# Two of the four blocks of v as seven block products, with gate blocks in their places, in a decoder layer

## The chip, the cores and the metric

The kernel runs on one core of one Trainium2 chip. The metric is the device time of one execution in microseconds (us), median of three runs; lower is better. The engines are called as the profile calls them: PE is TensorE (matmul), PEld its weight load, DVE VectorE, ACT ScalarE, POOL GpSimd, SP SyncE, which only issues DMAs here.

## The reference

One layer over x of 1024 tokens x 1024 channels, float32:

```
h = rms_norm(x, attn_norm_w)
q, k, v, u, g = split(h @ w_in)              # 1024, 1024, 1024, 2048, 2048 columns
q, k = rms_norm over each half head of 64    # 8 heads, two halves each
lam = exp(sum(lam_q1 * lam_k1)) - exp(sum(lam_q2 * lam_k2)) + lam_init
p = softmax(q1 k1' + bias) - lam * softmax(q2 k2' + bias)      # causal
y_a = (rms_norm(p @ v) * (1 - lam_init)) @ w_proj_attn
c = causal depthwise convolution of width 31 of (u_a * sigmoid(u_b))
y_b = silu(layer_norm(c)) @ w_proj_conv
x = x + (sigmoid(g_a) * y_a + sigmoid(g_b) * y_b) @ w_out
x = x + (silu(gate) * up) @ w_down           # gate, up from rms_norm(x), 2816 wide
```

## The kernel before

Every float32 matrix is split into a high part (rounded by ScalarE, `split_hi`, L120) and a low part (the rest, by VectorE in `split_lo`, L125, or by GpSimd in `low`, L131, while `low_by_pool` is set), and a product is three matmuls: high x high, high x low, low x high (L168 to L170). The projection of h is cut into items. `V0` to `V3` are the four blocks of 256 columns of v: per tile of 128 tokens 8 x 3 = 24 matmuls of 256 columns. `G0` to `G15` are blocks of 128 columns of the gates: per half of 512 tokens 24 matmuls of 512 columns. `Q0` to `Q7` are a head's q and k together, 256 columns like a V item. `U0` to `U7` are the convolution's input, two blocks of 128 columns each.

The program has stages. The **opening** (`opening`, from L1076) loads the tiles of x, normalises and turns them by matmuls with the identity (`turn_x`, L724), and does V0 and U0 in between. Its first instructions are three dummy matmuls (`keep_busy`, L208), the squares of the first tile in two halves (L699 on ScalarE, L700 on VectorE), the spreading of the norm's weight over the partitions by a matmul with a row of ones (L212, copied by L213), the norm (L714), three dummies again, and the split of V0's weights, which come in two DMAs of 512 KB (L1085). The lists `first` and `last` (L402, L403) then order the items: V1, V2 (`first`), then U1 to U7, then Q0, V3 (`last`). GpSimd sums the halves of h meanwhile into four matrices T1 to T4 (`sums_of_h`). The pairs U1 to U7 (`u_pair`) take their blocks by Winograd's form of Strassen's product: seven products of half-sized blocks (A11, A12, S1 to S4, A22 of the weights with h's quarters and T1 to T4) in place of eight, with the same weights prepared by `prepare` one item ahead, as a generator that is stepped between products.

**Attention** follows: 8 heads x 8 slots (`scores`, `turn`, `weigh`), and the lists in `later` say which items fill TensorE in which head: Q of the next head and one or two gate blocks; a generator is advanced by one group (an accumulation of one bank) per slot, and a head whose list has only one gate block leaves two slots without one. The convolution's 30 multiply-adds per block (`conv_taps`, L594, VectorE) run in the background: the loop at L1231 gives them 3.25 instructions per step of the first stage, and attention shares out the rest by its slack. q and k of a head are normalised over 64 channels (`rsq`: ScalarE's square root and VectorE's reciprocal for the first head, logarithm and exponential for the others), turned by TensorE (`turn_qk`, L815, named pQ) and partly moved between partitions by small DMAs (ks, qs; L826 to L837) before the first score (L1289, named sc). `make_neglam` computes lambda by an exponential at the start of attention, behind a load of ScalarE's table.

The rest of the layer (projections, layer norm, output product, feed-forward) is not touched. Tiles live in pools with rotating buffers, and the order of the instructions on each engine is fixed when the program is built, by a scheduler that starts from the order of the code.

## Time and profile before

| | |
|---|---|
| runs | 1730.33, 1729.57, 1726.5 us; median 1729.57 |
| the profiled execution's own time | 1735.99 us |
| its span, first to last instruction | 1734.2 us |
| mean granted TensorE clock | 0.998 |
| busy | PE 1718.1, PEld 1480.7, DVE 1286.8, ACT 862.0, POOL 219.1 us |
| opening, V1 starts at | 65.97 us |
| U pairs end, Q0 and V3 | 258.98 us |
| first score | 315.08 us |
| last score | 807.5 us |

The page gives the busy time of each engine and its share of the span. A row of the timeline has the start, the duration of the group, the engine, the line of the kernel, the operation, what it writes and reads, how many instructions it merges, and in brackets how long the engine had been idle and what ended that. A row of the windows view gives, for a stretch of the span, the busy microseconds of PE, PEld, DVE, ACT and POOL, each with its count of instructions, then the granted clock of TensorE, the share of the DMA engines and GB/s. A busy TensorE is not one at its peak: neighbouring matmuls overlap, so the pace is read from starts.

### The profile page before, as it was taken

What the parts mean: (1) busy time and instruction counts of PE and PEld (TensorE: products, weight loads), DVE (VectorE), ACT (ScalarE), POOL (GpSimd) and SP (SyncE); (2) the same over time, 40 slices, a digit from 0 to 9 for tenths busy, and PEclk for the clock granted to TensorE, in tenths of its full rate; (3) what the DMA queues carried; (4) which work ended last, traced back from release to release, by engine and by line L of the source; (5) the groups of instructions that cost most, each with busy time, mean ns of one, the idle gap of its engine ahead of it and who ended that gap; (6) DMA issues with size and microseconds to landing.
All of it is one profiled execution on the core that took longest, in us unless ns stands there. A gap on an engine that the chain in (4) does not pass through costs nothing.

```text
span 1734.2 us, 25866 instructions
## 1 busy us (share of the span) xinstructions
PE 1718.1 (99%) x9245; PEld 1480.7 (85%) x9245; DVE 1286.8 (74%) x2128; ACT 862.0 (50%) x1958; POOL 219.1 (13%) x207
## 2 busy tenths in 40 slices
PE   9899999999999999999999999999999999999999
PEld 7897889998998998988788888888888888888887
DVE  6785889898988888978587768966676667565554
ACT  5234334667777776755557324633333333333332
POOL 3988761000000000000000000000000000000000
PEclk9999999999999999999999999999999999999999
DMA  6244436436335444434973674235445444598663
GB/s 207 80 134 129 151 109 173 122 86 180 108 103 169 114 127 126 116 114 132 333 262 110 212 266 142 78 114 172 153 162 174 154 149 154 172 361 283 218 216 131
DMA packets 261603, 281.64 MB, mean 162 GB/s; under 512 B 16545, under 2 KB 181985, under 8 KB 261474
## 3 DMA queue, kind: packets, MB, share of 16 engines
q1 hardware_dynamic: 255360, 269.28, 48.1%
q0 software_dynamic: 5680, 9.39, 2.7%
q8 instruction: 73, 1.20, 0.3%
q10 hardware_dynamic: 434, 1.32, 0.2%
q14 instruction: 56, 0.46, 0.1%
HBM read 181.84 MB, written 85.50 MB: 154 GB/s over the span
## 4 chain that ended last, share of the span: by engine, by line
PE 94%; DVE 3%; DMA 2%; ACT 1%; issue 1%; SPq 0%; DVEq 0%; ACTq 0%
PE acc L980 30%; PE acc L488 12%; PE pg L168 12%; PE pg L169 12%; PE pg L170 12%; PE wo L1850 4%; PE sc L1289 2%; PE sc L1290 2%; PE pT L1328 2%; DVE acc L594 1%; PE pg L1106 1%; PE pW L168 1%; PE pW L169 1%; PE pW L170 1%; PE pQ L815 1%
## 5 line engine op out<-in xcount | busy, mean ns | idle before, releaser
L594 DVE SCALAR_TENSOR_TENSOR acc<-u,cw,acc 128x1023 f32<-128x1023 f32 (+14 forms) x240 | 303.4, 1264 | 25.2 <-ACT acc L588 22.6
L169 PE MATMUL pg<-wlo,hT_hi 128*128 128x256 f32 x704 | 200.9, 286 | 5.0 <-DVE wlo L125 5.0
L170 PE MATMUL pg<-whi,hT_lo 128*128 128x256 f32 x704 | 201.4, 286 | 0.0
L168 PE MATMUL pg<-whi,hT_hi 128*128 128x256 f32 x704 | 200.8, 286 | 0.4 <-DVE v L125 0.4
L125 DVE TENSOR_TENSOR wlo<-draw,whi 128x1024 fp32r<-128x1024 f32 x75 | 91.8, 1223 | 85.0 <-ACT whi L120 79.9
L120 ACT CAST whi<-draw 128x1024 fp32r<-128x1024 f32 x75 | 79.1, 1055 | 129.5 <-PE acc L488 116.0
L169 PEld LDWEIGHTS pg<-wlo,hT_hi 128*128 128x128 f32 x704 | 135.5, 192 | 7.3 <-DVE wlo L125 5.6
L168 PEld LDWEIGHTS pg<-whi,hT_hi 128*128 128x128 f32 x704 | 135.2, 193 | 2.1 <-DVE v L125 0.6
L170 PEld LDWEIGHTS pg<-whi,hT_lo 128*128 128x128 f32 x704 | 135.5, 192 | 1.7
L120 ACT CAST whi<-wraw 128x1024 fp32r<-128x1024 f32 x90 | 94.6, 1052 | 80.0 <-PE pg L169 31.1
L488 PE MATMUL acc<-wlo,whi 128*128 128x512 f32 x308 | 119.8, 389 | 0.0
L488 PE MATMUL acc<-whi,wlo 128*128 128x512 f32 x308 | 119.8, 389 | 0.0
L1296 ACT ACTIVATE E<-E,mn 128x640 f32<-128x640 f32 (+7 forms) x128 | 99.8, 781 | 30.5 <-DVE mn L1291 28.9
L168 PE MATMUL pg<-hT_hi,whi 128*128 128x512 f32 x288 | 114.4, 397 | 0.1
L169 PE MATMUL pg<-hT_lo,whi 128*128 128x512 f32 x288 | 113.7, 395 | 0.0
L170 PE MATMUL pg<-hT_hi,wlo 128*128 128x512 f32 x288 | 113.7, 395 | 0.0
L120 ACT CAST whi<-s 128x1024 fp32r<-128x1024 f32 x54 | 56.8, 1053 | 104.7 <-PE acc L980 101.7
L125 DVE TENSOR_TENSOR wlo<-wraw,whi 128x1024 fp32r<-128x1024 f32 x75 | 94.6, 1264 | 11.4 <-ACT whi L120 11.2
L1291 DVE CUSTOM_DVE_ANT_0 E<-sc,tb 128x512 f32<-128x512 f32 (+3 forms) x128 | 74.2, 585 | 33.3 <-PE pT L1328 16.0
L980 PE MATMUL acc<-h_hi,whi 128*128 128x512 f32 x240 | 93.4, 389 | 0.0
L980 PE MATMUL acc<-h_lo,whi 128*128 128x512 f32 x240 | 93.4, 389 | 0.0
L980 PE MATMUL acc<-h_hi,wlo 128*128 128x512 f32 x240 | 90.1, 389 | 0.0
(370 smaller groups left out, 4599.6 us busy)
## 6 DMA issues: line engine op xcount, KB each, us to landing
wraw<-in_w_gate_up_dram SPq DMA_DIRECT2D x44, 512.0 KB, 4.8
wraw<-in_w_in_dram SPq DMA_DIRECT2D x40, 512.0 KB, 4.1
qs<-qs SPq DMA_DIRECT2D x96, 128.0 KB, 2.3
wd<-in_w_down_dram SPq DMA_DIRECT2D x44, 256.0 KB, 3.2
tdT<-wd SPq DMA_DIRECT2D x88, 128.0 KB, 4.6
draw<-sdS SPq DMA_DIRECT2D x44, 256.0 KB, 3.8
draw<-tdT SPq DMA_DIRECT2D x44, 256.0 KB, 3.9
wraw<-in_w_in_dram SPq DMA_DIRECT2D x32, 256.0 KB, 3.3
```

The costliest lines, as they stand in the source:

```text
L120: act.copy(dst, src)
L125: last_lo[0] = dve.tensor_tensor(dst, src, f32(hi), op=ALU.subtract).ins
L168: pe.matmul(o, lh, rh, start=start, stop=False)
L169: pe.matmul(o, lh, rl, start=False, stop=False)
L170: last_mm[0] = pe.matmul(o, ll, rh, start=False, stop=stop).ins
L488: m = pe.matmul(o[s_][i][:], l_[:, ts], r_[:, 512:], start=start and j + y_ == 0, stop=j == n - 1 and y_ == 2, skip_group_check=not start,)
L594: dve.scalar_tensor_tensor(a_, us[c][:, : S - n], cw[:, c, t : t + 1], a_, op0=ALU.mult, op1=ALU.add)
L980: last_mm[0] = pe.matmul(o[:], a_[x_][:, k, :], b_[y_][:, k, :], start=start and k + x_ + y_ == 0, stop=k == 3 and x_ == 1, skip_group_che ...
L1289: pe.matmul(o[:, :w], qh[:, qs], k, start=True, stop=False)
L1291: dve.tensor_tensor_reduce(e[:, ks], o[:, :w], tb[:, S - nk + c0 : S - nk + c0 + w], 1.0, mn[:, j : j + 1] if c0 else 3.0e38, ALU.add, ALU ...
L1296: act.activation(e[:, :nk], e[:, :nk], AF.Exp, bias=mn[:, j : j + 1], scale=-1.0, accum_out=l[:, j : j + 1])
L1850: last_mm[0] = pe.matmul(o[s_][i][:], A[u_], B[v_], start=start and j + y_ == 0, stop=j == 3 and y_ == 2, skip_group_check=not start,).ins
```

## The change

Five things change.

- V2 and V3 leave the lists. `wide_pair` computes both together behind U7 as seven products of 512 tokens x 512 rows x 256 columns (`tall`), with weights from `wide_prepare` and the T matrices that the U pairs already use. Six PSUM banks serve as three pairs; ScalarE copies three partial sums out (L1091 of the changed kernel), VectorE adds three times two halves (L1098), and all eight halves are split and stored as before.
- G0 and G1 take V2's place in `first`, G2 and G3 take V3's in `last`; in attention each of the seven heads with a Q item has one gate block.
- The convolution's background steps are 3.0 per product in `wide_pair` and 1.5 per step of G2 and G3.
- V0's weights and the second tile of x are issued from ScalarE's queue, and one dummy matmul stands where the second three stood.
- The first head's q and k use logarithm and exponential; the logarithm's table is loaded, and lambda computed, ahead of Q0.

On ScalarE the program starts so before (xt is a tile of x, wraw the weights of V0, anw_b the norm's weight):

```order
L185 ACT_TABLE_LOAD
L199 DMA anw_b<-in_attn_norm_w_dram 1x1024
L202 DMA xt_102<-in_x_dram 128x512
L699 ACTIVATE xj_349,ssx_348<-xt_102 128x512
L190 DMA xt_354<-in_x_dram 128x1024
L190 DMA xt_356<-in_x_dram 128x1024
L652 ACTIVATE t_361<-v_358 128x1
```

and so after the change, on the same engine at the same place:

```order
L185 ACT_TABLE_LOAD
L199 DMA anw_b<-in_attn_norm_w_dram 1x1024
L202 DMA xt_102<-in_x_dram 128x512
L1187 DMA wraw_334<-in_w_in_dram 128x4x256
L1187 DMA wraw_335<-in_w_in_dram 128x4x256
L190 DMA xt_338<-in_x_dram 128x1024
L690 ACTIVATE xj_349,ssx_348<-xt_102 128x512
L190 DMA xt_354<-in_x_dram 128x1024
```

Three DMAs have come from SyncE's queue to stand between the first tile's second half and ScalarE's first squares.

On VectorE, behind the last U pair (its last operation is L1021 here), the program before goes on with taps of the convolution and then the roots of Q0 (L682):

```order
L1015 TENSOR_TENSOR u_259_2471<-acc_2412,u_259_2471 128x512
L1021 TENSOR_TENSOR p_252_2425<-acc_2411,p_252_2425 128x512
L594 SCALAR_TENSOR_TENSOR acc_2407<-u_2060,cw,acc_2407 128x1023
L594 SCALAR_TENSOR_TENSOR acc_2407<-u_2060,cw,acc_2407 128x1022
L594 SCALAR_TENSOR_TENSOR acc_2407<-u_2060,cw,acc_2407 128x1021
```

After the change the seven products stand there; this is the piece around the adds that the product with T4 waits for (acc_2447 and acc_2448 are the bank pair of S3, u_279 and u_280 the partial sums, wvh a high part; L585 is a tap):

```order
L585 SCALAR_TENSOR_TENSOR acc_2297<-u_1950,cw,acc_2297 128x1010
L585 SCALAR_TENSOR_TENSOR acc_2297<-u_1950,cw,acc_2297 128x1009
L1098 TENSOR_TENSOR u_279_2628<-acc_2447,u_279_2628 128x512
L585 SCALAR_TENSOR_TENSOR acc_2297<-u_1950,cw,acc_2297 128x1008
L125 TENSOR_TENSOR u_279_2628<-u_279_2628,wvh_2743 128x512
L585 SCALAR_TENSOR_TENSOR acc_2297<-u_1950,cw,acc_2297 128x1007
L1098 TENSOR_TENSOR u_280_2629<-acc_2448,u_280_2629 128x512
L585 SCALAR_TENSOR_TENSOR acc_2297<-u_1950,cw,acc_2297 128x1006
L1098 TENSOR_TENSOR u_283_2687<-acc_2451,u_283_2687 128x512
```

Adds and splits are now mixed with taps, one tap between each two.

On TensorE, the program before goes from U7 (L980, with T3) over to Q0 (L168 to L170):

```order
L980 MATMUL acc_2411<-T3l,whi_2397 128x512
L980 MATMUL acc_2411<-T3h,wlo_2398 128x512
L168 MATMUL pg_2564<-whi_2444,hT_hi 128x256
L169 MATMUL pg_2564<-wlo_2445,hT_hi 128x256
L170 MATMUL pg_2564<-whi_2444,hT_lo 128x256
```

After the change, this is the place in the seven products where the one with T2 (S2) ends and S4 and S3 (with T3) go on by turns:

```order
L1074 MATMUL acc_2448<-wlo_2506,T2h 128x256
L1074 MATMUL acc_2451<-whi_2632,hT_hi 128x256
L1074 MATMUL acc_2451<-whi_2632,hT_lo 128x256
L1074 MATMUL acc_2447<-whi_2573,T3h 128x256
L1074 MATMUL acc_2447<-whi_2573,T3l 128x256
L1074 MATMUL acc_2447<-wlo_2574,T3h 128x256
```

Two matmuls of S4 now stand between S2 and S3, which share a bank pair.

The diff:

```diff
--- before.py
+++ after.py
@@ -399,19 +399,10 @@
 
 
 
-    first = ["V1", "V2"]
-    last = ["Q0", "V3"]
-    later = [
-        ["Q1", "G0", "G1"],
-        ["Q2", "G2", "G3"],
-        ["Q3", "G4"],
-        ["Q4", "G5", "G6"],
-        ["Q5", "G7"],
-        ["Q6", "G8", "G9"],
-        ["Q7", "G10"],
-        ["G11", "G12", "G13", "G14"],
-        ["G15"],
-    ]
+    first = ["V1", "G0", "G1"]
+    last = ["Q0", "G2", "G3"]
+    later = [["Q1", "G4"], ["Q2", "G5"], ["Q3", "G6"], ["Q4", "G7"], ["Q5", "G8"], ["Q6", "G9"], ["Q7", "G10"]]
+    later += [["G11", "G12", "G13", "G14"], ["G15"]]
 
     def loads_of(it):
         c = int(it[1:])
@@ -802,7 +793,7 @@
                     )
                 if i2 == 0:
                     yield
-            r = rstd_of(ss[:], 16, 1.0 / HD, fast=h > 0)
+            r = rstd_of(ss[:], 16, 1.0 / HD, fast=True)
             r4 = raw[:].rearrange("p i (g d) -> p (i g) d", d=HD)
             dve.tensor_tensor(r4, r4, r.unsqueeze(2).to_broadcast([P, 16, HD]), op=ALU.mult)
 
@@ -1026,6 +1017,122 @@
         yield
         return nxt
 
+    def wide_prepare(items):
+
+
+        raws = {}
+        for z, (c, j) in {"11": (0, 0), "12": (0, 1), "21": (1, 0), "22": (1, 1)}.items():
+            if c:
+                raws[z] = st[0].tile([P, 1024], F32, tag="s12" if j == 0 else "s34", name=nm("wide"), bufs=1)
+            else:
+                raws[z] = wraw()
+            c0 = V0 + 256 * items[c]
+            nc.sync.dma_start(
+                raws[z][:].rearrange("p (k c) -> p k c", c=256),
+                win[512 * j : 512 * (j + 1), c0 : c0 + 256].rearrange("(k p) c -> p k c", p=P),
+            )
+        A = {}
+
+        def parts(z, raw):
+            A[z] = [[t_[:, 256 * k : 256 * (k + 1)] for k in range(4)] for t_ in wsplit(raw)]
+
+        def less(o, a_, b_):
+            pool.tensor_tensor(raws[o][:], raws[a_][:], raws[b_][:], op=ALU.subtract)
+
+        yield
+        parts("11", raws["11"])
+        yield A
+        less("11", "11", "21")
+        pool.tensor_tensor(raws["21"][:], raws["21"][:], raws["22"][:], op=ALU.add)
+        parts("12", raws["12"])
+        yield
+        A["22"] = [], []
+        for g in range(2):
+            v = raws["22"][:, 512 * g : 512 * (g + 1)]
+            hi, lo = [st[0].tile([P, 512], F32R, tag=t_, name=nm(t_), bufs=2) for t_ in ("sh", "sl")]
+            split_hi(hi[:], v)
+            low(lo[:], v, hi[:])
+            for t_, list_ in zip((hi, lo), A["22"]):
+                list_.extend(t_[:, 256 * e : 256 * (e + 1)] for e in range(2))
+        parts("S1", raws["21"])
+        less("22", "22", "11")
+        less("12", "12", "22")
+        yield
+        for z, raw in (("S2", "22"), ("S3", "11"), ("S4", "12")):
+            parts(z, raws[raw])
+            yield
+        ws.ahead = 1
+        ws.fetch()
+        yield
+
+    def tall(o2, a_, b_, start):
+
+        for i in range(4):
+            ts, dst = slice(i * P, (i + 1) * P), o2[i // 2][:, 256 * (i % 2) : 256 * (i % 2 + 1)]
+            for k in range(4):
+                for x_, y_ in ((0, 0), (0, 1), (1, 0)):
+                    last_mm[0] = pe.matmul(
+                        dst, b_[y_][:, k, ts], a_[x_][k], start=start and i % 2 + k + x_ + y_ == 0,
+                        stop=k == 3 and x_ == 1, skip_group_check=not start or i % 2 == 1,
+                    ).ins
+
+    def wide_pair(items, A, ahead):
+
+        B = {(j, l): (hT_hi[:, KH[j], TOK[l]], hT_lo[:, KH[j], TOK[l]]) for j in range(2) for l in range(2)}
+        x = [acc() for _ in range(6)]
+        b, a, c_ = x[0:2], x[2:4], x[4:6]
+
+        def room(tag):
+            return st[0].tile([P, 512], F32R, tag=tag, name=nm(tag), bufs=1 if tag == "u2" else 2)[:]
+
+        def copies(tags, o2):
+            t2 = [room(tag) for tag in tags]
+            for t_, o_ in zip(t2, o2):
+                act.copy(f32(t_), o_[:])
+            return t2
+
+        def out(t2, c, l, o2=None):
+            for e, t_ in enumerate(t2):
+                v = f32(t_)
+                if o2 is not None:
+                    dve.tensor_tensor(v, o2[e][:], v, op=ALU.add)
+                else:
+                    v, t_ = t_[:], room("u3")
+                hi = wp.tile([P, 512], F32R, tag="sg", name=nm("wvh"), bufs=2)[:]
+                split_hi(hi, v)
+                split_lo(t_, v, hi)
+                rows_ = slice(256 * (2 * l + e), 256 * (2 * l + e + 1))
+                for t3, dst in ((hi, v_hi[items[c]]), (t_, v_lo[items[c]])):
+                    nc.sync.dma_start(
+                        dst[rows_, :].rearrange("(e p) c -> p e c", p=P), f32(t3).rearrange("p (e c) -> p e c", c=256)
+                    )
+
+        tall(b, A["11"], B[0, 0], True)
+        p1 = copies(("p1", "p1"), b)
+        next(ahead)
+        yield 3.0
+        tall(a, A["12"], B[1, 0], True)
+        out(p1, 0, 0, a)
+        next(ahead)
+        yield 3.0
+        tall(c_, A["S1"], TS[1], True)
+        u3 = copies(("u3", "u3"), c_)
+        next(ahead)
+        yield 3.0
+        tall(b, A["S2"], TS[2], False)
+        u2 = copies(("u2", "p1"), b)
+        yield 3.0
+        tall(b, A["S3"], TS[3], False)
+        out(u3, 1, 1, b)
+        next(ahead)
+        yield 3.0
+        tall(c_, A["S4"], B[1, 1], False)
+        out(u2, 0, 1, c_)
+        yield 3.0
+        tall(b, A["22"], TS[4], False)
+        out(b, 1, 0)
+        yield 3.0
+
     def first_stage():
 
 
@@ -1033,12 +1140,6 @@
         tsum = sums_of_h()
         yield from opening()
         ups = [prepare(win, (U0 + D + c * P, U0 + c * P), st[0], 2, c == 1) for c in range(1, NKT)]
-
-        def weights_ahead():
-            yield
-            ws.ahead = 1
-            ws.fetch()
-            yield
 
         for n, _ in enumerate(run(first)):
             if n < 5:
@@ -1057,36 +1158,37 @@
                 next(ups[0])
             yield
         for c in range(1, NKT):
-            ahead = ups[c] if c < NKT - 1 else weights_ahead()
+            ahead = ups[c] if c < NKT - 1 else wide_prepare((2, 3))
             next(ahead)
             A = yield from u_pair(c, A, ahead)
+        yield from wide_pair((2, 3), A, ahead)
         st_ctx.close()
         tt_ctx.close()
         ff_ctx.close()
         qkp = qk_ctx.enter_context(tc.tile_pool(name="qkp", bufs=2, side="right", reuse_waits="tile"))
         apl.append(at_ctx.enter_context(tc.tile_pool(name="attn", bufs=2, reuse_waits="tile")))
 
-        def v3_tiles():
-            t_ = apl[0].tile([P, 1024], F32R, tag="E", name=nm("v3"), bufs=4)
-            return t_[:, :512], t_[:, 512:]
-
-        v_tiles[0] = v3_tiles
         load_bias(0)
         ws.ahead = 2
+        last_act = last_of(mybir.EngineType.Activation)
+        with after(last_act):
+            tc.keep_in_program_order(act.preload_act_table_set("natural_log_exp_and_others"))
+            make_neglam()
         yield from run(last[:1])
         bg.until((NKT - CONV_PSUM) * (CW + 1) - 1)
-        yield from run(last[1:])
+        for _ in run(last[1:]):
+            yield 1.5
 
     def opening():
 
 
         raws = [wraw(), wraw()]
         for g, raw in enumerate(raws):
-            nc.sync.dma_start(
+            nc.scalar.dma_start(
                 raw[:].rearrange("p (k c) -> p k c", c=256),
                 win[512 * g : 512 * (g + 1), V0 : V0 + 256].rearrange("(k p) c -> p k c", p=P),
             )
-        xload(1)
+        xload(1, nc.scalar)
         wv = [[vw.tile([P, 1024], F32R, tag=t_, name=nm(t_)) for t_ in ("vwh", "vwl")] for g in range(2)]
         halves = [[t_[:].rearrange("p (k c) -> p k c", c=256) for t_ in w] for w in wv]
         uw, o = [], {}
@@ -1125,7 +1227,7 @@
             lambda: spread_weights(0),
             lambda: spread_weights(1),
             lambda: norm(0),
-            lambda: keep_busy(3),
+            lambda: keep_busy(1),
             lambda: wv_hi(0),
             lambda: split_lo(wv[0][1][:], raws[0][:], wv[0][0][:]),
             lambda: turn_x(0, (0,)),
@@ -1231,7 +1333,7 @@
     bias_anchor = []
     n = 0
     due = 0.0
-    for _ in first_stage():
+    for taps in first_stage():
         n += 1
         if n in (18, 19, 20):
             with after(bias_anchor[0]):
@@ -1239,7 +1341,7 @@
         if n >= 23 and n % 3 == 2 and (n - 23) // 3 < 2:
             with after(last_of(mybir.EngineType.Pool)):
                 bias_skew((n - 23) // 3)
-        due += 3.25
+        due += taps or 3.25
         with after(last_of(mybir.EngineType.DVE)):
             bg.step(int(due))
         due -= int(due)
@@ -1376,11 +1478,6 @@
             at = aps.tile([P, 512], F32, tag="at", name=nm("at"), bufs=2)
             act.activation(at[:], pt[:], AF.Identity, scale=pcol("subln"))
             nc.sync.dma_start(a_d[h][:, sb * 512 : (sb + 1) * 512], at[:])
-
-    last_act = last_of(mybir.EngineType.Activation)
-    tc.keep_in_program_order(act.preload_act_table_set("natural_log_exp_and_others"))
-    with after(last_act):
-        make_neglam()
 
     inatt[0] = True
     load_v(0)
```

## The prediction

> **What bounds the kernel now.** I began with the page's busy times and its chain, to see which engine sets the end.

> ```profile
> span 1734.2 us, 25866 instructions
> PE 1718.1 (99%) x9245; PEld 1480.7 (85%) x9245; DVE 1286.8 (74%) x2128; ACT 862.0 (50%) x1958; POOL 219.1 (13%) x207
> PE 94%; DVE 3%; DMA 2%; ACT 1%; issue 1%; SPq 0%; DVEq 0%; ACTq 0%
> ```

> TensorE is busy 99% of the span and carries 94% of the chain that ended last. So a matmul removed is time removed, unless TensorE then waits. Next the waits of TensorE, longest first:

> ```profile
> PE pg L169 <- DVE wlo L125: 5.0, 2, 4.2
> PE sc L1289 <- DMA ks<-klo: 1.5, 2, 1.2
> PE pm L208 <- DVE busy L195: 1.5, 1, 1.5
> PE sc L1289 <- DVE mn L1291: 0.6, 1, 0.6
> ```

> Only one long wait is left: 5.0 us for a weight's low part, at the first weights of V1. Last, three stretches of the windows view, which give the pace of a matmul:

> ```profile
> 86.00:96.00 10.00, 10.00 (x86) 10.00 (x85) 9.86 (x9) 3.98 (x6) 5.54 (x3) 1.00 0.58 180
> 190.00:200.00 10.00, 10.00 (x46) 8.28 (x45) 9.59 (x9) 2.76 (x4) 7.46 (x6) 1.00 0.55 166
> 71.00:78.00 7.00, 6.21 (x31) 5.91 (x29) 3.27 (x2) 1.04 (x1) 7.00 (x3) 0.52 0.63 187
> ```

> The count includes matmuls cut by the window's edges, about two. In V's code 84 matmuls of 256 columns take 10 us, 0.119 us each; in U's pairs 44 of 512 columns, 0.227 us each. The group view's 286 and 389 ns are longer, because neighbouring matmuls overlap; they must not be multiplied. The third row is the stretch behind the long wait: granted clock 0.52, so about half of its 7 us is lost (7 x 0.48 = 3.4).

> **Step 1, the seven products.** V2 and V3 are 2 x 8 token tiles x 24 = 384 matmuls of 256 columns; the seven products are 7 x 4 x 12 = 336 of the same shape. 48 fewer, 48 x 0.119 = **5.7 us off** TensorE. The gate blocks G0 to G3 keep all their matmuls and only change place: 4 x 48 x 0.227 = 43.6 us leave attention and come to stand where V2 and V3 stood. On TensorE that sums to nothing.

> What must hide beside the seven products, which last 336 x 0.119 = 40.0 us:

> ```profile
> L594 DVE SCALAR_TENSOR_TENSOR acc<-u,cw,acc 128x1023 f32<-128x1023 f32 (+14 forms) x240 | 303.4, 1264 | 25.2 <-ACT acc L588 22.6
> 297.14 0.68 DVE L125 TENSOR_TENSOR v<-pg,v 128x512 fp32r<-128x512 f32 x1
> L131 POOL TENSOR_TENSOR wlo<-s,whi 128x1024 fp32r<-128x1024 f32 x14 | 34.0, 2435 | 13.7 <-ACT whi L120 13.7
> 256.50:315.00 58.50, 58.14 (x476) 57.48 (x475) 49.99 (x56) 30.27 (x105) 12.68 (x9) 1.00 0.68 190
> ```

> VectorE has, between the last U pair and its last split, 22 taps x 1.26 + 6 adds and 8 splits x 0.68 = 37 us (an add of 512 columns is not in the trace in this form; I take the split of equal size). That fits in 40 with little to spare; in the stretch of Q0 and V3 it was 50 of 58.5. GpSimd makes three low parts of 2.4 us, the two loads of Q0 as many, and two differences of that size: 17 us. ScalarE has 14 casts and copies of about 0.6 us and five of 1.05: under 15 us. The tightest hand-over is the product with T4: it adds onto the bank pair that VectorE has to read after S3. In between TensorE has 38 matmuls of S4 and, for the second bank, 24 of T4's own: 62 x 0.119 = 7.4 us of cover for one add of 0.68 us and what is queued ahead of it. Without that cover every microsecond of lateness is idle TensorE. Bounds: nothing, and 14 us (rival 3); I take **0.4 us lost**, near the row of V3, where TensorE idled 0.36 us of 58.5.

> **Step 2, the opening.** Rows of the first 11 us, in order of time:

> ```profile
> 0.74 0.39 SPq L202 DMA_DIRECT2D xt<-in_x_dram  x1
> 1.19 0.97 SPq L1085 DMA_DIRECT2D wraw<-in_w_in_dram  x2
> 1.33 0.37 ACTq L202 DMA_DIRECT2D xt<-in_x_dram  x1
> 2.20 0.50 SPq L190 DMA_DIRECT2D xt<-in_x_dram  x1
> 3.13 3.75 PE L212 MATMUL pm<-anw_b,one 1*128 1x512 f32 x4
> 3.70 0.63 ACT L699 ACTIVATE xj<-xt 128x512 f32<-128x512 f32 x1 [1.68 <-DMA xt<-in_x_dram]
> 5.54 0.69 DVE L700 CUSTOM_DVE_ANT_0 xj<-xt 128x512 f32<-128x512 f32 x1 [4.01 <-DMA xt<-in_x_dram]
> 6.73 0.20 ACT L652 ACTIVATE t<-v 128x1 f32<-128x1 f32 x1 [2.31 <-DVE v L682]
> 6.84 1.05 ACT L213 COPY anw_b<-pm 128x512 f32<-128x512 f32 x2
> 7.46 1.65 PE L208 MATMUL pm<-busy 128*128 128x512 f32 x3 [0.58 <-ACT anw_b L213]
> 8.01 1.41 DVE L714 SCALAR_TENSOR_TENSOR xt<-xt,r,anw_b 128x512 f32<-128x512 f32 x2
> 8.90 1.94 PE L724 MATMUL px<-ident,xt 128*128 128x128 f32 x8
> 10.66 0.58 PE L1106 MATMUL pg<-vwh,hT_hi 128*128 128x256 f32 x1
> ```

> The second half of the first tile was issued 0.59 us after the first half but landed 1.84 us after it, since SyncE's two weight loads started in between. With these and the second tile behind it on ScalarE's queue, it should land about 3.70 + 0.59 = 4.3, so VectorE starts 1.25 us earlier. The three issues cost ScalarE's queue 0.97 + 0.50 us from 1.70 on, done at 3.2, ahead of the 3.70 at which it needs to square: hidden. The weight row's spread (L212) still ends at 6.88, so the second copy ends at 7.5; the norm then runs at 6.7 and 7.5, not at 8.01 and 8.7. Two dummies of 0.48 us fewer leave TensorE free for the transposes. I take **1.2 us off**; the ends are 1.3 off (the whole landing) and 0.5 on (weights that land later than they are wanted).

> [...]

> **Step 3, the first scores.** The roots of the first head by logarithm and exponential, and lambda's logarithm table ahead of Q0, take a table load and a reciprocal away from engines that have room; I cost them at nothing. But V3 used to stand between the second turning of q and k and the first score:

> ```profile
> 298.96 1.03 PE L815 MATMUL pQ<-ident,qkraw 128*128 128x128 f32 x8
> 300.67 0.74 DVE L824 SCALAR_TENSOR_TENSOR klo<-pQ,pvec,ks 128x512 fp32r<-128x512 f32 x1
> 302.04 1.25 SPq L837 DMA_DIRECT2D ks<-klo  x1
> DMA to landing us min/median/max: 2.2/2.4/4.6
> 315.08 0.40 PE L1289 MATMUL sc<-ks,qs 128*128 128x512 f32 x1
> ```

> Then 16.1 us, of which k needed 302.04 + 2.4 - 298.96 = 5.5, at most 7.7. Now 17 gate matmuls and 27 of Q1 stand there: 0.8 + 17 x 0.227 + 27 x 0.119 = 7.9 us. So the wait lies between nothing and some 2 us (two or three taps more ahead on VectorE); I take **0.4 us lost**, near the two waits of 1.5 us in all at other heads.

> **Step 4, attention with less matmul work.** Two stretches of the size of a head, the first mostly of a head with two gate blocks, the second of one with one block:

> ```profile
> 381.00:446.00 65.00, 64.85 (x433) 59.16 (x434) 56.24 (x126) 48.80 (x161) 3.59 (x11) 1.00 0.55 149
> 446.00:507.00 61.00, 61.00 (x448) 57.78 (x448) 54.43 (x125) 45.90 (x158) 1.45 (x8) 1.00 0.38 107
> ```

> VectorE is busy 87% and 89%, and TensorE idles in neither. All seven heads become like the second. VectorE also loses work: 17 taps (103 instead of 120 after the first score in program order) and four low parts. I cost it at nothing; the ends are 2 us either way.

> **The sum**, against the profiled execution (1735.99 us, 1734.2 of it the span): - 5.7 - 1.2 + 0.4 + 0.4 = -6.1, so 1729.9. The median of the runs shown is 1729.57, 6.4 under the profiled one; the same difference gives **1723.5 us**.

> **The rivals.** Rival 1: the long wait goes. Its rows:

> ```profile
> 49.74 14.19 DVE L272 TENSOR_TENSOR lprod<-lamt 128x64 f32<-128x64 f32 x1
> 56.72 7.12 POOL L905 TENSOR_TENSOR F<-F,F 128x1024 f32<-128x1024 f32 x3
> 62.90 1.04 ACT L120 CAST T1h<-F 128x1024 fp32r<-128x1024 f32 x1
> 64.61 2.37 POOL L922 TENSOR_TENSOR T1l<-F,T1h 128x1024 fp32r<-128x1024 f32 x1 [0.76 <-ACT T1h L120]
> 70.41 0.39 PE L169 MATMUL pg<-wlo,hT_hi 128*128 128x256 f32 x1 [4.17 <-DVE wlo L125]
> ```

> A product of 64 columns stood on VectorE for 14.19 us, until GpSimd's run of tensor operations ended at 63.84 and GpSimd waited for a cast that ended at 63.94. Only in that gap did VectorE get through, and V1's weights came late. The order of these operations on both engines is unchanged, so I keep the wait. But the gap hangs on 0.1 us: if GpSimd's run ends a microsecond earlier against the cast, most of 5.0 us of waiting and 3.4 of half clock go, up to 8.4: 1715 us. If it ends later, the wait grows by one operation, 2.4 us: 1726 us (rival 4).

> [...]

> Rival 3, the slower side: VectorE falls behind in the seven products. Six of its splits there read two operands of SBUF while GpSimd works; L272 shows what can come of that, and one operation of GpSimd is 2.4 us, so 6 x 2.4 = 14.4 us late at worst, 7.4 of it covered. The 7.0 idle then cost 3.4 of half clock more, as at 71: 1723.5 + 10.4 = 1734. It makes the kernel slower from about 13 us late on, five to six splits held. Against it: GpSimd has 17 us of work in 40, so most splits meet it idle. [...]

> That the change doesn't do what it says is excluded: the matmul rows of the built program are 48 fewer.

> **How the numbers follow.** Forecast (1719.5 to 1726): 0.57. Rival 1: 0.12. Rival 2: 0.11. Rival 4: 0.09. Rival 3: 0.11. A measurement can tell about 0.2%, 3.5 us: below 1726.1 is faster. That takes the forecast, rival 1, half of rival 2: 0.74; rival 4 and the rest of 2 are the same: 0.15; rival 3 is slower: 0.11. The range leaves out rival 3 and the far end of rival 1: 1714 to 1730.

> **What would show it.** Step 1: between the last U pair and Q0, 336 matmuls in about 40 us at clock 1.00, no wait of TensorE over 1 us. Step 2: the squares of VectorE start near 4.3 and the first V matmul near 9.3. Step 3: a wait for the k transfer at the first score under 1 us. Step 4: attention 43 us shorter with VectorE under 92%. I would be wrong by a long wait at T4's product or at the first score, or by another length of the wait near 66 us.

## The result, and the profile after

The changed kernel takes **1732.62 us** (median of 10 runs, 1730.56 to 1735.16); the kernel before takes 1728.26 beside it (10 runs, 1726.45 to 1730.33). The ratio is **1.0026, 95% interval 1.0018 to 1.0034**: about 4.5 us slower, where 1723.5 was forecast. The profiled execution took 1731.95 us. From its page, the span, the busy times and the shares of the chain that ended last:

```profile
span 1730.2 us, 25791 instructions
PE 1713.0 (99%) x9195; PEld 1475.8 (85%) x9195; DVE 1284.9 (74%) x2128; ACT 865.6 (50%) x1969; POOL 247.1 (14%) x219
PE 90%; DMA 3%; DVE 3%; ACT 2%; issue 1%; POOL 1%; SPq 0%; POOLq 0%; DVEq 0%; ACTq 0%
```

TensorE's busy time is 5.1 us lower than in the profile of before (some of either is matmuls at half clock), and yet the runs got longer. In the chain DMA now has 3% and GpSimd 1%. TensorE's waits of the same execution:

```profile
PE sc L1391 <- DMA ks<-klo: 3.4, 2, 2.5
PE sc L1392 <- DMA qs<-qs: 1.4, 1, 1.4
PE sc L1391 <- DVE mn L1393: 1.1, 2, 0.9
PE pQ L806 <- DVE qkraw L798: 1.0, 1, 1.0
```

The 5.0 us for a weight's low part are gone and waits in the hand-over of q and k have come. The long wait's cause, the product of 64 columns (L272), reads so in the changed kernel:

```profile
49.42 4.76 DVE L272 TENSOR_TENSOR lprod<-lamt 128x64 f32<-128x64 f32 x2
```

Two of them took 4.76 us in all; in the profile of before the first alone took 14.19. The opening's rows (the squares of the first tile's second half, its transposes, the first matmul of V0):

```profile
5.22 0.69 DVE L691 CUSTOM_DVE_ANT_0 xj<-xt 128x512 f32<-128x512 f32 x1 [3.69 <-DMA xt<-in_x_dram]
8.58 1.94 PE L715 MATMUL px<-ident,xt 128*128 128x128 f32 x8 [0.65 <-DVE xt L705]
10.34 1.01 PE L1208 MATMUL pg<-vwh,hT_hi 128*128 128x256 f32 x3
```

Each comes only 0.32 us earlier than before. The windows row of the seven products:

```profile
247.40:287.70 40.30, 40.30 (x328) 39.85 (x327) 36.96 (x33) 16.13 (x23) 25.54 (x12) 1.00 0.56 166
```

TensorE is never idle in them, at full clock, for 40.3 us (40.0 were forecast for the 336 matmuls; some records are missing). VectorE has 37 us of work there, as forecast.

### The profile page after: what moved, and what is told of

It reads as the page before. It is cut to its first block, busy times and chain, and to the rows that moved or that the text cites. A ratio compares the mean times of both kernels' runs of the same rounds, so it can differ in the third digit from the quotient of the medians.

```text
span 1730.2 us, 25791 instructions
## 1 busy us (share of the span) xinstructions
PE 1713.0 (99%) x9195; PEld 1475.8 (85%) x9195; DVE 1284.9 (74%) x2128; ACT 865.6 (50%) x1969; POOL 247.1 (14%) x219
## 4 chain that ended last, share of the span: by engine, by line
PE 90%; DMA 3%; DVE 3%; ACT 2%; issue 1%; POOL 1%; SPq 0%; POOLq 0%; DVEq 0%; ACTq 0%
PE acc L971 28%; PE acc L479 12%; PE pg L168 11%; PE pg L169 11%; PE pg L170 11%; PE wo L1947 3%; PE acc L1074 2%; PE sc L1392 2%; PE sc L1391 2%; PE pT L1430 2%; PE pg L1208 1%; DVE acc L585 1%; PE pW L170 1%; PE pW L168 1%; PE pW L169 1%
## 5 line engine op out<-in xcount | busy, mean ns | idle before, releaser
L585 DVE SCALAR_TENSOR_TENSOR acc<-u,cw,acc 128x1023 f32<-128x1023 f32 (+14 forms) x240 | 305.8, 1274 | 14.1 <-ACT acc L579 11.2
L168 PE MATMUL pg<-whi,hT_hi 128*128 128x256 f32 x576 | 165.0, 286 | 0.0
L170 PE MATMUL pg<-whi,hT_lo 128*128 128x256 f32 x576 | 164.8, 286 | 0.0
L169 PE MATMUL pg<-wlo,hT_hi 128*128 128x256 f32 x576 | 164.3, 285 | 0.0
L125 DVE TENSOR_TENSOR wlo<-draw,whi 128x1024 fp32r<-128x1024 f32 x75 | 91.7, 1224 | 83.0 <-ACT whi L120 73.4
L120 ACT CAST whi<-draw 128x1024 fp32r<-128x1024 f32 x75 | 79.1, 1055 | 129.5 <-PE acc L479 121.0
L120 ACT CAST whi<-wraw 128x1024 fp32r<-128x1024 f32 x90 | 94.8, 1054 | 74.9 <-PE pg L169 30.2
L168 PE MATMUL pg<-hT_hi,whi 128*128 128x512 f32 x288 | 113.9, 395 | 0.1
L169 PE MATMUL pg<-hT_lo,whi 128*128 128x512 f32 x288 | 113.5, 394 | 0.0
L170 PE MATMUL pg<-hT_hi,wlo 128*128 128x512 f32 x288 | 113.3, 394 | 0.0
L168 PEld LDWEIGHTS pg<-whi,hT_hi 128*128 128x128 f32 x576 | 110.5, 192 | 2.1 <-ACT jk L791 0.2
L169 PEld LDWEIGHTS pg<-wlo,hT_hi 128*128 128x128 f32 x576 | 110.3, 192 | 1.5
L120 ACT CAST whi<-s 128x1024 fp32r<-128x1024 f32 x54 | 56.9, 1053 | 109.0 <-PE acc L971 101.6
L170 PEld LDWEIGHTS pg<-whi,hT_lo 128*128 128x128 f32 x576 | 110.2, 191 | 1.3
L125 DVE TENSOR_TENSOR wlo<-wraw,whi 128x1024 fp32r<-128x1024 f32 x71 | 88.4, 1247 | 10.2 <-ACT whi L120 9.9
```

Source lines behind the costliest of these rows:

```text
L120: act.copy(dst, src)
L125: last_lo[0] = dve.tensor_tensor(dst, src, f32(hi), op=ALU.subtract).ins
L168: pe.matmul(o, lh, rh, start=start, stop=False)
L169: pe.matmul(o, lh, rl, start=False, stop=False)
L170: last_mm[0] = pe.matmul(o, ll, rh, start=False, stop=stop).ins
L585: dve.scalar_tensor_tensor(a_, us[c][:, : S - n], cw[:, c, t : t + 1], a_, op0=ALU.mult, op1=ALU.add)
```

## The experiments

Ratios are to the kernel before, with 95% intervals; their own table stands at the end. Two letters change their meaning in the expectations as the theories did: A, later H, holds that TensorE waits in the hand-over of q and k; V that VectorE's amount of work sets the time. **One number in them is wrong**: VectorE "0.99 busy" in the score stage was summed from groups of the timeline, whose durations hold gaps. The windows view, which counts busy time alone, gives 0.86. V is judged below with that number.

**1. The kernel before, profiled again.** No edit.

> The kernel before, unchanged, profiled a second time. Theory A holds that the profiled execution from which the prediction was made had a stall that the kernel seldom has: one VectorE subtraction (L272) of 14.19 us near 66 us, behind which TensorE stood 4.2 us and then ran at a granted clock of 0.5. By A, the new execution has no L272 over 10 us near 66 us, the second block product of v starts without a wait, and the profiled time is near 1727.6 (1735.99 less 8.4). The rival, that the kernel always has this stall and the changed kernel took it away, expects the 14 us subtraction again and a profiled time of 1734 to 1737.

One run, 1727.89 us, span 1726.1. The row of L272 in it:

```profile
50.85 4.78 DVE L272 TENSOR_TENSOR lprod<-lamt 128x64 f32<-128x64 f32 x2
```

No stall and no wait behind it. The profile that the prediction rests on held a stall which neither this execution nor any other profiled one here had. Its 1735.99 us stood 5.7 above the slowest of ten runs for that reason. Of 96 further runs of the kernel before, taken beside the experiments, one took 1735.18 us at a granted clock of 0.998; it was not traced, so whether it held the same stall is open.

**2. The opening alone.**

```diff
-            nc.sync.dma_start(
+            nc.scalar.dma_start(
...
-        xload(1)
+        xload(1, nc.scalar)
...
-            lambda: keep_busy(3),
+            lambda: keep_busy(1),
```

> The kernel before with the first tile's second half and the first weights on ScalarE's queue and one dummy product run in place of three: the change's opening and nothing else. Theory A (the loss stands behind the first stage): 0.3 us faster, that is 1728 and not to be told from no change, with the start of the first block product of v 0.3 us earlier. The prediction's own step 2 gave -1.2, 1727.1. Rival B (the other queue order delays later loads, which then cost the first stage): slower by 1 to 4 us, 1729 to 1732.

1.0002 (0.9993 to 1.0011): by all runs, nothing that can be measured. But two of the twelve took 1733.65 and 1732.87 us at a granted clock of 0.998, as the stalled profile of before did; the other ten have a mean of 1726.4 us, 1.0 below the 1727.3 of the kernel before. The traces say the same. The landing that the step counted on varies by about 1 us: the second half reached VectorE at 5.54 to 6.72 us in the seven profiled executions here with the old opening (mean 6.2) and at 4.67 to 5.71 in the thirteen with the new one (mean 5.0). V1 starts at 66.6 and 65.5 us in the mean. So the new opening gives about 1.2 us.

**3. The gate blocks moved, v left as it was.**

```diff
-    last = ["Q0", "V3"]
+    last = ["Q0", "V3", "G0", "G1", "G2", "G3"]
+    later = [["Q1", "G4"], ["Q2", "G5"], ["Q3", "G6"], ["Q4", "G7"], ["Q5", "G8"], ["Q6", "G9"], ["Q7", "G10"]]
+    later += [["G11", "G12", "G13", "G14"], ["G15"]]
...
+        for _ in run(last[2:]):
+            yield 1.75
```

> The kernel before with four gate blocks ahead of the first score, in steps of 1.75 taps, and one in each head after it, as in the changed kernel; items 2 and 3 of v stay plain blocks, so the matmul work is that of before. Theory A (the heads lose the matmul work that covered the hand-over of q and k): slower by 4 to 7 us, 1732 to 1735, and waits for the q and k tiles' DMAs in the score stage. The first score itself has the third item of v and four blocks ahead of it, so it should not wait as in the changed kernel. Rival B (the loss comes from what the seven products load on VectorE and the queues, not from where the gates stand): within 1 us of before, 1727 to 1729.

**1.0046** (1.0034 to 1.0058), 8.0 us slower with no matmul more or less. So moving gate blocks, with the taps that move along, can cost more than the whole change. But it is mostly not the heads with one block that cost it here. The longest wait stands right behind the first score (L585 is a tap, mn VectorE's running minimum of the scores):

```profile
324.53 22.89 DVE L585 SCALAR_TENSOR_TENSOR acc<-u,cw,acc 128x1017 f32<-128x1017 f32 x16
348.08 0.48 PE L1282 MATMUL sc<-ks,qs 128*128 128x128 f32 x1 [3.41 <-DVE mn L1284]
347.23:354.06 6.83, 5.98 (x26) 5.88 (x27) 6.83 (x16) 2.18 (x5) 0.00 (x0) 0.50 0.28 79
```

Sixteen taps stood in a row on VectorE, TensorE waited 3.41 us for the minimum behind them, and its clock was then at half for 6.83 us, which is 3.4 more. The changed kernel, with another pace of taps, has no such wait, so the two runs can't be subtracted to price the rest of the change. A's waits for the transfers of k are 1.1 us in all. The stretch from the first score to the last projection's first matmul (the score stage below) in the second execution of before, in this kernel and in the changed one:

```profile
308.14:822.62 514.48, 513.01 (x3414) 468.46 (x3413) 441.75 (x978) 364.52 (x1198) 19.41 (x73) 1.00 0.44 126
```

```profile
340.26:831.75 491.49, 483.48 (x3306) 445.83 (x3304) 421.51 (x961) 360.63 (x1203) 18.41 (x72) 0.99 0.43 122
```

```profile
341.50:827.34 485.84, 480.68 (x3277) 442.73 (x3278) 419.33 (x958) 355.02 (x1200) 18.51 (x72) 0.99 0.44 124
```

Length less PE's busy time is TensorE's idle time: 1.5 us before, 8.0 and 5.2 in the two others, whose granted clock is also below 1.

**4. The changed kernel with its taps later.**

```diff
-        yield from run(last[:1])
+        for _ in run(last[:1]):
+            yield 2.0
...
-            yield 1.5
+            yield 0.25
```

> The changed kernel with another spread of the convolution's taps: 2.0 in each step of the first query block in place of 3.25, and 0.25 in each step of the two gate blocks before the first score in place of 1.5, so that fewer of VectorE's 5.2 us taps stand ahead of the subtraction that makes the low part of k. Theory A1 (the first score waits because VectorE's queue holds taps ahead of that subtraction): the waits of 1.0 and 2.5 us there go, 3 us faster than the changed kernel if the left-over taps cost nothing in the heads, about 1729.5; up to 1 us of it comes back where the taps meet the heads' work. Rival (the wait is set by the DMA of k and its chain, not by the taps): 1732 to 1733, with the wait before the first score as before.

1.0030 (1.0020 to 1.0040): no gain. The first score itself no longer waits (it starts at 336.85 us, 4.7 earlier; the turning ahead of it waits 1.6 us), but the five taps that it pushed into the score stage cost there what was won: 7.9 us of idle TensorE.

**5 and 6. Both kernels with half the taps.**

```diff
             def go():
+                if t and t % 2 == 0:
+                    return
                 n = CW - 1 - t
```

> The kernel before with 14 of the convolution's 30 VectorE taps of each block left out (so the convolution's result is not the reference's); all of TensorE's work stays. This takes about 70 us of VectorE's work out of the score stage, where 120 taps take 151 us, and as much out of the stage ahead. Theory V (the score stage is bound by VectorE, busy 0.99 of it): TensorE's lost time of 20 us there falls by half or more, 10 to 16 us faster than the kernel before, 1712 to 1718. Theory A (the time is lost in the hand-over of q and k through ScalarE, VectorE and the DMAs when too little matmul work stands beside it, whatever VectorE has to do): 0 to 4 us faster, 1723 to 1728.

> The changed kernel with the same 14 of 30 taps of each block left out (the convolution's result is not the reference's). It is read against the kernel before with the same taps left out. Theory V: with VectorE's load gone the 5.7 us of matmul work that the seven products save come through, and this one is 5 to 7 us faster than the other, near 1708. Theory A: where the gate blocks stand still matters, and this one is 2 to 6 us slower than the other, as the full kernels are. A result in between would say that both have a part.

0.9982 (0.9973 to 0.9991), 1724.25 us, and **0.9942** (0.9929 to 0.9956), **1717.71 us**. With less work on VectorE the changed kernel is 6.5 us faster than the other, near the 5.7 of the seven products and the 1.2 of the opening together. Its score stage:

```profile
334.47:813.48 479.01, 477.67 (x3306) 442.60 (x3304) 367.89 (x908) 356.73 (x1201) 18.35 (x72) 1.00 0.45 127
```

1.3 us idle. So the waits need VectorE's load; with that load gone the gates' place costs nothing. The kernel before gained only 3.5, less than V asked: at 0.86 it is not bound by VectorE.

**7 and 8. One normalisation given to ScalarE.**

```diff
-        dve.tensor_tensor(an[:], an[:], r.unsqueeze(2).to_broadcast([P, NT, VD]), op=ALU.mult)
+        for i in range(NT):
+            act.activation(an[:, i, :], an[:, i, :], AF.Identity, scale=r[:, i : i + 1])
```

> The kernel before with one piece of VectorE's work in the score stage given to ScalarE: the normalisation of a head's output, one VectorE instruction of 1.22 us a head, 8.5 us in seven heads, becomes eight ScalarE instructions a head with a scale by row, near 0.37 us each, 21 us in all on an engine that is busy 0.71 of that stage. Theory V: 5 to 8 us faster than the kernel before, 1720 to 1723. Theory A: no change, 1727 to 1729, or slower where ScalarE's row of eight delays a copy that TensorE waits for.

> The changed kernel with the same normalisation by ScalarE. Theory V: 5 to 8 us faster than the changed kernel, 1724.5 to 1727.5, that is within 0.2% of the kernel before and 3 to 5 us slower than the kernel before with the same edit. Theory A: 1732 to 1733, as the changed kernel.

0.9999 (0.9990 to 1.0008) and 1.0043 (1.0030 to 1.0055). V fails for both. The second is confounded, since ScalarE has more to do in it and TensorE may wait for that (2.8 us of its waits in that profile end with ScalarE's jk, ph, at and ar; in the changed kernel's 0.5). Hence the next pair, without ScalarE.

**9 and 10. The normalisation left out, and done twice.** The line above is deleted in the changed kernel, or doubled in the kernel before.

> The changed kernel with the normalisation of each head's output by VectorE left out (one instruction of 1.22 us a head, 8.5 us in the seven heads of the score stage; the output is then not the reference's) and nothing put in its place on ScalarE. Theory V (VectorE's total of work sets the length of the score stage): 5 to 8 us faster than the changed kernel, 1724.5 to 1727.5. Theory S (the loss is made in single steps, where a row of scores has no gate or query block beside it and VectorE falls behind for that step; the total counts for little): 0 to 3 us faster, 1729.5 to 1732.6.

> The kernel before with the same instruction run twice in each head (8.5 us more work for VectorE in the score stage; the output is then not the reference's). Theory V: VectorE was busy for 0.99 of that stage, so the time grows by 5 to 8 us, 1733 to 1736. Theory S: 0 to 3 us slower, 1728 to 1731.

1.0031 (1.0019 to 1.0042): 8.5 us less work for VectorE, no gain. 1.0051 (1.0038 to 1.0063): 8.5 us more, 8.8 us slower, as V held for this one. Taken together this is neither a total nor a proportion. It looks as if the kernel before stands next to an edge and the changed one beyond it, but these two runs alone don't show that.

**11. Other steps left bare.**

```diff
-        return 0 if plan[n // NT] == 6 and n % NT in (4, 6) or n == len(steps) - 1 else 1
+        return 0 if plan[n // NT] == 6 and n % NT in (5, 7) or n == len(steps) - 1 else 1
```

> The changed kernel with one pair of numbers changed: a head that has one gate block has matmul work beside six of its eight steps, and the two bare steps are moved from the fifth and seventh (128 and 384 keys) to the sixth and eighth (256 and 512 keys). By the kernel's own estimate of a step, TensorE runs out 0.92 and 1.35 us before VectorE in the old bare steps and 0.49 and 0.28 us before it in the new, 1.5 us a head over seven heads. Theory S: TensorE's waits in the score stage shrink by half, 4 to 8 us faster than the changed kernel, 1724.5 to 1728.5. Theory V (VectorE's total): no change, 1732 to 1733.5, since nothing of VectorE's work goes.

**1.0070** (1.0057 to 1.0083): S, and V too, wrong; the slowest of all. A head now ends without a gate block, and the longest wait is

```profile
PE sc L1391 <- DMA qs<-qs: 4.9, 1, 4.9
```

at 697 us, the end of the sixth head. This speaks for the matmul work beside the hand-over at a head's end, and against the estimate of slack.

**12. The last weights split by VectorE.**

```diff
+        low_by_pool[0] = False
         yield from run(last[:1])
```

> The changed kernel with the last three weights that GpSimd splits ahead of the first score (10.8 us of GpSimd near 311 to 326 us, beside which two VectorE instructions of 0.2 us take 2.37 us and one tap takes 3.41 us) split by VectorE in 1.22 us each. VectorE then has 3.7 us more to do and 6.5 us less to stand. Theory of the lock: the waits at the first query block's turning and at the first score shrink from 3.5 us to 0 to 2, and the kernel is 2 to 4 us faster than the changed kernel, 1728.5 to 1730.5. Rival (the taps queued ahead set these waits, not the lock): 1732 to 1734.

**0.9999** (0.9991 to 1.0008): about 4.7 us off the changed kernel, level with the kernel before. (Four splits leave GpSimd, not three; the profiled execution, 1729.09 us, is the slowest of its eleven.) What happened ahead of the first score in the changed kernel:

```profile
323.65 2.63 POOL L131 TENSOR_TENSOR wlo<-wraw,whi 128x1024 fp32r<-128x1024 f32 x1 [7.18 <-ACT whi L120]
323.94 2.37 DVE L647 TENSOR_SCALAR t<-t 128x16 f32<-128x16 f32 x1
329.35 1.21 DVE L798 TENSOR_TENSOR qkraw<-qkraw,r 128x1024 f32<-128x1024 f32 x1
330.70 1.23 PE L806 MATMUL pQ<-ident,qkraw 128*128 128x128 f32 x8 [1.01 <-DVE qkraw L798]
331.14 5.18 DVE L585 SCALAR_TENSOR_TENSOR acc<-u,cw,acc 128x1013 f32<-128x1013 f32 x4
336.24 0.74 DVE L815 SCALAR_TENSOR_TENSOR klo<-pQ,pvec,ks 128x512 fp32r<-128x512 f32 x1
338.20 0.60 SPq L828 DMA_DIRECT2D ks<-klo  x1
341.50 0.71 PE L1391 MATMUL sc<-ks,qs 128*128 128x512 f32 x1 [2.46 <-DMA ks<-klo]
```

A VectorE instruction on 16 columns (0.17 us alone) stands 2.37 us beside GpSimd's split, and another did so at 314.13. So the normalised q and k come late, their turning (pQ) waits, and then four taps stand between the turning and the low part of k. With the split on VectorE:

```profile
323.54 1.22 DVE L798 TENSOR_TENSOR qkraw<-qkraw,r 128x1024 f32<-128x1024 f32 x1
325.81 5.20 DVE L585 SCALAR_TENSOR_TENSOR acc<-u,cw,acc 128x1015 f32<-128x1015 f32 x4
329.98 1.03 PE L806 MATMUL pQ<-ident,qkraw 128*128 128x128 f32 x8
331.34 0.75 DVE L815 SCALAR_TENSOR_TENSOR klo<-pQ,pvec,ks 128x512 fp32r<-128x512 f32 x1 [0.33 <-ACT ks L813]
337.99 0.40 PE L1392 MATMUL sc<-ks,qs 128*128 128x512 f32 x1
```

The same four taps now stand ahead of the turning, where nobody waits.

**13. The same edit in the kernel before,** as its control.

> The kernel before with the same edit: the weights that GpSimd splits behind the seventh pair of products are split by VectorE (three of 2.4 us there). It is the control of the 5 us that this gave the changed kernel. If the lock was a loss that the change brought on: no change, 1727 to 1728.5, since in the kernel before none of these splits stood beside an instruction of the first head's factors. If the edit is a gain by itself: 2 to 5 us faster, 1722.5 to 1725.5.

1.0025 (1.0016 to 1.0035): slower by 4.3 us, which neither expected. So the edit is no gain by itself. In the kernel before TensorE then waits for ScalarE's squares at 375 and 390 us, where the second head begins, and the clock drops once; how the edit leads there is not shown. The waits are:

```profile
PE pg L168 <- ACT jk L800: 3.6, 2, 2.0
```

**14 and 15. Taps away from a head's end; bare steps at the sixth and seventh place** (both on top of the split by VectorE).

```diff
+    slack = [s_ * (0.25 if n_ % NT in (5, 7) else 1.0) for n_, s_ in enumerate(slack)]
```

```diff
-        return 0 if plan[n // NT] == 6 and n % NT in (4, 6) or n == len(steps) - 1 else 1
+        return 0 if plan[n // NT] == 6 and n % NT in (5, 6) or n == len(steps) - 1 else 1
```

> The changed kernel with its last weights split by VectorE, and in the score stage three quarters of the taps of a head's sixth and eighth step moved to its other steps; the number of taps is the same. It is read against the changed kernel with the split alone (1.0002 of the kernel before... 0.9999 measured). Theory H (taps queued on VectorE ahead of the hand-over of q and k at a head's end make TensorE wait there, and its granted clock then drops to about 0.5 for 3.4 us): the wait near 697 us and its clock drop go, 3 to 6 us faster than with the split alone, 1721.5 to 1724.5. Theory V (only the amount of VectorE's work counts): no change, 1726.5 to 1728.5; if the fuller early steps fall behind instead, up to 1731.

> The changed kernel with its last weights split by VectorE, and the two bare steps of a head with one gate block moved from the fifth and seventh to the sixth and seventh, so that the block's matmuls stand in the fifth and the eighth: beside the first turning of q and at the head's end. Theory H: the hand-over has matmul work beside both of its ends, 1 to 4 us faster than with the split alone, 1723.5 to 1726.5. Theory V: no change, 1726.5 to 1728.5. The run with the bare steps at the sixth and eighth place was 7.6 us slower than the changed kernel, so a head that ends bare costs; this one ends as before.

1.0032 (1.0020 to 1.0044) and 1.0018 (1.0009 to 1.0027): 3 to 6 us slower than the split alone, where H expected gains. The wait near 692 us stayed in both (1.8 and 2.1 us). H in the form "taps queued ahead of the hand-over" falls.

**16 and 17. A second gate block given back to heads that wait** (again on top of the split by VectorE).

```diff
-    later = [["Q1", "G4"], ["Q2", "G5"], ["Q3", "G6"], ["Q4", "G7"], ["Q5", "G8"], ["Q6", "G9"], ["Q7", "G10"]]
-    later += [["G11", "G12", "G13", "G14"], ["G15"]]
+    later = [["Q1", "G4"], ["Q2", "G5"], ["Q3", "G6"], ["Q4", "G7"], ["Q5", "G8"], ["Q6", "G9", "G10"], ["Q7", "G11"]]
+    later += [["G12", "G13", "G14"], ["G15"]]
```

> The changed kernel with its last weights split by VectorE, and one gate block moved from the last head to the sixth, at whose end (692 us) every version with one block there waits for q or k and loses half its clock for 3.4 us. Theory H (a head that ends with too little matmul work waits in the hand-over): that wait and clock drop go, 3 to 5 us faster than with the split alone, 1722.5 to 1725, and faster than both kernels. Theory V (the amount of VectorE's work): no change, 1726.5 to 1728.5. If the last head, now with two bare steps, waits instead, up to 1731.

> The same, with a second block in the second head as well (its end is near 455 us, where the version with the split alone waits 2.5 us and drops its clock once), so that the last head has two blocks and four bare steps. Theory H: 2 to 4 us faster than the run with one block moved where the last head can bear it, 1719 to 1722.5; the last head, with 22 us less of matmul work, may give back 3 to 8 of it, 1724 to 1730. Theory V: 1726 to 1729.

**0.9995** (0.9986 to 1.0003), 1726.54 us, the lowest ratio of a kernel that computes the whole layer, but not to be told from the kernel before; and 1.0046 (1.0028 to 1.0065). The wait at 692 us shrank to 0.5 us and its clock drop went, as H said, in the first: the stretch there is

```profile
695.00:700.00 5.00, 4.47 (x36) 4.17 (x35) 4.70 (x12) 1.89 (x6) 0.00 (x0) 1.00 0.92 186
```

But the last head, a block poorer, waits between 787 and 799 us for VectorE and ScalarE, and in the second kernel drops its clock near 772. The wait is moved more than removed.

**18. The changed kernel with a quarter of the taps out.**

```diff
             def go():
+                if t and t % 4 == 0:
+                    return
                 n = CW - 1 - t
```

> The changed kernel with 7 of the convolution's 30 taps of each block left out (the result is then not the reference's), some 24 of 103 taps or 30 us of VectorE's work in the score stage, so that VectorE is busy for about 0.93 of it. Leaving out 14 gave 14.9 us. If the waits need a full VectorE (a threshold near 0.97): nearly all of it comes already, 10 to 14 us faster than the changed kernel, 1718.5 to 1722.5. If they shrink with the work in proportion: 6 to 8.5 us, 1724 to 1726.5.

**0.9964** (0.9949 to 0.9979), 10.6 us faster than the changed kernel: seven tenths of the gain of 6 for half of its edit. That is not one edge in the score stage, though. Between the profiled executions, 8.3 us apart, the first score starts 7.8 us earlier, 3.2 of it because 27 matmuls of 256 columns now come behind it. The score stage is as long as in the changed kernel with these 27 in it. VectorE was at 0.80 there, not 0.93; TensorE idles 6.5 us, more than the 5.2, but none of the waits drops the clock, which is 3.4. Only with half of the taps out does the idle time go.

| kernel | ratio | score stage, us | TensorE idle | clock lost | VectorE busy |
|---|---|---|---|---|---|
| before, again | - | 514.5 | 1.5 | 0 | 0.86 |
| before, opening alone | 1.0002 | 514.9 | 1.9 | 0 | 0.86 |
| before, norm by ScalarE | 0.9999 | 514.4 | 1.7 | 0 | 0.85 |
| before, norm twice | 1.0051 | 519.3 | 5.5 | 0 | 0.87 |
| before, split by VectorE | 1.0025 | 516.1 | 5.9 | 1.8 | 0.86 |
| before, half the taps | 0.9982 | 522.8 | 1.2 | 0 | 0.75 |
| before, gates moved | 1.0046 | 491.5 | 8.0 | 3.5 | 0.86 |
| changed | 1.0026 | 485.8 | 5.2 | 3.4 | 0.86 |
| changed, taps later | 1.0030 | 489.5 | 7.9 | 1.7 | 0.87 |
| changed, norm by ScalarE | 1.0043 | 489.3 | 8.8 | 1.8 | 0.84 |
| changed, no norm | 1.0031 | 486.7 | 7.5 | 1.8 | 0.84 |
| changed, bare steps 6 and 8 | 1.0070 | 490.9 | 9.7 | 5.1 | 0.86 |
| changed, split by VectorE | 0.9999 | 485.1 | 5.8 | 3.4 | 0.87 |
| changed, split by VectorE, taps away from a head's end | 1.0032 | 489.4 | 8.5 | 5.1 | 0.86 |
| changed, split by VectorE, bare steps 6 and 7 | 1.0018 | 486.5 | 8.8 | 1.7 | 0.86 |
| changed, split by VectorE, second block in head 6 | 0.9995 | 485.0 | 6.4 | 0 | 0.86 |
| changed, split by VectorE, second block in heads 2 and 6 | 1.0046 | 491.7 | 9.9 | 3.4 | 0.86 |
| changed, quarter of the taps out | 0.9964 | 485.4 | 6.5 | 0 | 0.80 |
| changed, half of the taps out | 0.9942 | 479.0 | 1.3 | 0 | 0.77 |

Idle is the stage's length less PE's busy time in the windows view; clock lost is the sum over stretches of 5 us of 5 x (1 - granted clock).

## Why the prediction was wrong, step by step

**The base.** The rows of the long wait were read rightly (49.74 to 63.93 us, 5.0 waited, 3.4 of half clock), but not what they said of the base: the execution was 6.4 us above the median because of this stall. Carrying the offset over made the sum right again, but rival 1, "up to 8.4: 1715", then took away a loss that nearly all runs don't have. No run showed a gain there.

**Step 1 held.** The changed kernel has 48 matmuls of 256 columns fewer, worth 5.7 us; the seven products ran without a wait and T4's product was covered. Rival 3 did not happen. Its 1734 lies near the measured time by luck, since its path (VectorE late in the seven products) was not taken.

**Step 2 held in size**: 1.2 us forecast, 1.2 in the mean of the profiled executions (experiment 2). But the squares did not start at 4.3. The 5.54 that the step was worked out from was the earliest of seven with the old opening, and the mean of the new one is 5.0; so between the two first profiles it was only 0.3. No run shows the loss of 1.7 us that rival 2 (0.11 of the chances) was put at: full clock began at 13.88 us in the first profile of the changed kernel and at 12.91 in that of before, and yet V1 started 1.1 us earlier in the mean of the executions with the new opening (experiment 2).

**Step 3 failed** at "the wait lies between nothing and some 2 us (two or three taps more ahead on VectorE)", of which 0.4 was taken. From V1's start to the first score the changed kernel takes 34.8 us longer than the second profile of before, for 192 matmuls of 512 columns more and 106 of 256 fewer, which by the paces of the prediction are worth 192 x 0.227 - 106 x 0.119 = 31.0: 3.8 lost. The wait's clock drop behind the first score cost 1.7 more:

```profile
341.00:346.00 5.00, 4.50 (x21) 4.15 (x22) 4.76 (x10) 0.53 (x1) 0.00 (x0) 0.66 0.66 174
```

5 x (1 - 0.66) = 1.7. Together 5.5, of which the split by VectorE gave 4.7 back. The term that was mis-sized is the time that k needs after its turning: 5.5 us, "at most 7.7", became 341.50 - 330.70 = 10.8. The cover of 7.9 was about right (10.8 less the 2.46 waited is 8.3). Four taps, 5.2 us, stood in the chain; GpSimd's split came ahead of it and made the turning itself late, for which TensorE waited 1.0.

**Step 4 failed**, at "VectorE is busy 87% and 89%, and TensorE idles in neither. All seven heads become like the second. ... I cost it at nothing; the ends are 2 us either way." Against the second profile of before, the score stage lost 8.0 us more than its matmuls are worth (28.6 us shorter by length; 192 matmuls of 512 columns fewer and 58 of 256 more are 192 x 0.227 - 58 x 0.119 = 36.7): 3.7 more idle, 3.4 of half clock (half of that behind the first score, counted in step 3), the rest slower pace. So 6.3 us were lost in the heads, where nothing was put. The two stretches quoted were read rightly, TensorE hardly idles in them. But that a one-block head ran well between two-block heads doesn't say that seven in a row do, and a stretch without idle time doesn't tell how near to a wait each hand-over is. Half the taps out showed that the loss needs VectorE's load. The run with the gate blocks moved alone does not price the heads, since 6.8 us of what its profile lost are the one wait behind its first score.

**The sum, with measured terms**, against the second profile of before (spans 1726.1 and 1730.2): start of V1 1.4 earlier, matmuls -5.7, up to the first score +3.8, score stage +8.0, behind it -0.6, together +4.1, as the spans differ. By this sum the kernel would be 1.4 us faster without the 5.5 of step 3, and 2.2 faster without the 6.3 of step 4. It took both to make it slower.

**What stays open.** Shown: with VectorE at 0.77 the waits go; at 0.84 to 0.87 every version with one block in each of seven heads idles 5 to 10 us, in single waits. In the changed kernel these are mostly for q and k at a head's end; with the gates moved alone, and with the bare steps at the sixth and seventh place, mostly for VectorE's minimum (4.7 and 4.5 us). A second block in the sixth head removes most of the wait there, and the last head then waits instead. Not settled: why 8.5 us less of VectorE's work doesn't help the changed kernel and 8.5 more costs the kernel before 8.8, and why moving the same taps away from a head's end makes it slower. That the kernel before sits on one good order among many poor ones fits all runs, but is only argued.

## What to carry to other kernels

Compare the profiled execution with all the runs before building on it: one 6 us above the median holds something the others lack, and the row to look for is one instruction much longer than its like. An engine at 0.86 can still be on the critical path; before filler work is moved out of a stage, look not at the stage's mean but at each hand-over it covered, and add what stands queued between its links. A change that is worth 7 us on TensorE can lose more than that where it alters what stands beside and ahead of the hand-overs of the other engines. And when a run is meant to price one part of a change, look in its profile for where its time went before taking the ratio as the price.
